# Stick-breaking attention in a four-layer trunk: the weight matrix taken as differences of one scan, the values as steps between neighbours

## The chip, the cores and the metric

The kernel runs on one core of one Trainium2 chip. The core has TensorE (PE, with its weight loads listed apart as PEld), VectorE (DVE), ScalarE (ACT), GpSimd (POOL) and the queue of SyncE (SP), which issues most of the transfers. The metric is the time of one execution in device microseconds (us); of several runs the median is taken.

## The reference

The program computes a trunk in float32 for a sequence of 1024 positions and a model width of 1024: a convolution layer, a gated feed-forward layer, an attention layer and a second feed-forward layer. The change touches the attention layer only. Its core, cut to what is computed:

```python
z = jnp.einsum("bhqd,bhsd->bhqs", q_blk, kf) * scale
valid = kpos[None, :] < qpos[:, None]
log_keep = jnp.where(valid, jax.nn.log_sigmoid(-z), 0.0)
rc = lax.cumsum(log_keep, axis=3, reverse=True)
after = jnp.concatenate([rc[..., 1:], jnp.zeros_like(rc[..., :1])], axis=-1)
weight = jnp.where(valid, jnp.exp(jax.nn.log_sigmoid(z) + after), 0.0)
return jnp.einsum("bhqs,bhsd->bhqd", weight.astype(v.dtype), v)
```

With keep = sigmoid(-z) and beta = sigmoid(z) = 1 - keep, a weight is beta at one key times the product of keep over all later keys before the query. There are 16 heads of width 64, and queries go in blocks of 128.

## The kernel before

All large tensors live in 1024-column slots of SBUF, given out by the class `Mem` from a first-in, first-out list. float32 products on PE are made from two rounded parts, a high part that ACT casts and a low part (value minus high part) that DVE subtracts; a full product is three matmuls (`mm3`).

Attention (`attention`, line 1384 on) works on pairs of heads, p = 0 to 7. For each pair there are these stages:

- `qkv_piece` multiplies 8 row tiles t by the pair's slice of the weights, 8 pieces k each. `qkv_split` prepares the next pair's weights: 8 casts on ACT (L1166) and 8 subtractions on DVE (L1167). `qkv_post` takes a finished tile out of PSUM: q and k by an ACT copy (L1190), the value part v by an ACT cast (L1193) and a DVE subtraction (L1194). `qkv_stat` squares on POOL (L1202), sums on DVE (L1203, then L709), takes a power on POOL (L710) and scales on POOL (L1212).
- `stacks` transposes q and k on PE (L1228) and splits the result: ACT L1234, DVE L1237.
- `z_part` makes the scores (L1260, L1261, and a mask matmul L1263). From PSUM, ACT writes keep (L1265) and beta (L1266).
- `z_scan` runs a product scan over keep, from the last key to the first, on DVE (L1274). `z_mul` multiplies beta by the scan, shifted by one column, on POOL (L1279).
- `a_bank` transposes the weights 128 by 128 on PE (L1293), casts the high part on ACT (L1297) and subtracts the low part on DVE (L1298). `av_bank` multiplies by v (L1312) and adds two halves (ACT L1322, DVE L1323).

The transposes of `stacks` and `a_bank` share two PSUM banks, called tr here. They take turns, so a transpose waits until the DVE instruction that reads the same bank two transposes earlier is done. The scores have two banks of their own.

What sets the order: PE's order in attention is written out by hand. Each step gets a time in units, 20 units to a pair, from tables at the end of `attention` (`ZT`, `ST`, `ZL` and others), and steps are issued in the order of these times. On DVE, ACT, POOL and SP a planner orders the instructions when the program is built, so a changed cost or dependence can move them. Each engine and each queue then works strictly in its order. After the tile t = 7 of a pair its v is complete; the first `av_bank` that reads it comes some 14 units later. Towards the end (`wo_start`) the output projection's weights are loaded and split beside the last pair, partly by POOL (L629 in `o_split`).

Of the kernel before, what the change touches and what calls it, by code (L numbers as in the profile page):

```python
# [618 lines left out]
class Kern:  # L619
# [563 lines left out]
    def qkv_post(self, p, t):  # L1183
        nc, m = self.nc, self.m
        ps = self.qps
        half, tl = divmod(t, 4)
        if tl == 0:
            self.qk[p, half] = m.alloc()
            self.V[p, half] = m.alloc()
        nc.scalar.copy(out=m.ap(self.qk[p, half])[:, tl * 256:(tl + 1) * 256], in_=ps[:, 0:256])  # L1190
        v = m.ap(self.V[p, half]).rearrange("p (t h c) -> p t h c", t=4, h=2)[:, tl]
        pv = ps[:, 256:384].rearrange("p (h c) -> p h c", h=2)
        nc.scalar.copy(out=r(v[:, :, 0:DH]), in_=pv)  # L1193
        nc.vector.tensor_tensor(out=r(v[:, :, DH:2 * DH]), in0=pv, in1=v[:, :, 0:DH], op=ALU.subtract)  # L1194
# [47 lines left out]
    def z_part(self, p, h, qb, c0):  # L1242
# [4 lines left out]
        if c0 == 0:  # L1247
            bs = m.alloc()
            if n <= 512:
                ks, B, K = None, m.ap(bs)[:, 0:n], m.ap(bs)[:, 512:512 + n]  # L1250
            else:
                ks = m.alloc()
                B, K = m.ap(bs)[:, 0:n], m.ap(ks)[:, 0:n]
            self.A[p, h, qb] = (bs, B, ks, K)
        _, B, _, K = self.A[p, h, qb]
# [8 lines left out]
        sc = DH ** -0.5  # L1264
        nc.scalar.activation(K[:, c0:c1], ps, AF.Sigmoid, scale=-sc)  # L1265
        nc.scalar.activation(B[:, c0:c1], ps, AF.Sigmoid, scale=sc)  # L1266
# [4 lines left out]
    def z_scan(self, p, h, qb):  # L1271
        K = self.A[p, h, qb][3]
        rev = K[:, 1:(qb + 1) * P][:, ::-1]
        self.nc.vector.tensor_tensor_scan(out=rev, data0=rev, data1=rev, initial=1.0, op0=ALU.mult, op1=ALU.bypass)  # L1274

    def z_mul(self, p, h, qb):
        bs, B, ks, K = self.A[p, h, qb]
        n = (qb + 1) * P
        self.nc.gpsimd.tensor_tensor(out=B[:, 0:n - 1], in0=B[:, 0:n - 1], in1=K[:, 1:n], op=ALU.mult)  # L1279
        if ks is not None:  # L1280
            self.m.free(ks)

    def a_bank(self, p, h, i, b):

        nc, m = self.nc, self.m
        q0, q1 = self.A[p, h, 2 * i], self.A[p, h, 2 * i + 1]
        ps = self.tr()
        pos, spans = 0, []
        for kb in (2 * b, 2 * b + 1):
            qs = (q0, q1) if kb <= 2 * i else (q1,)  # L1290
            spans.append((kb, pos, len(qs) * P))
            for q in qs:
                nc.tensor.transpose(ps[:, pos:pos + P], q[1][:, kb * P:(kb + 1) * P], self.ident)  # L1293
                pos += P
        s = m.alloc()
        aH, aL = m.ap(s)[:, 0:pos], m.ap(s)[:, 512:512 + pos]
        nc.scalar.copy(out=r(aH), in_=ps[:, 0:pos])  # L1297
        nc.vector.tensor_tensor(out=r(aL), in0=ps[:, 0:pos], in1=aH, op=ALU.subtract)  # L1298
        self.AT[p, h, i, b] = (s, spans)
        if b == i:  # L1300
            for q in (2 * i, 2 * i + 1):
                m.free(self.A.pop((p, h, q))[0])
# [81 lines left out]
    def attention(self):  # L1384
# [20 lines left out]
        for p in range(NP):  # L1405
# [16 lines left out]
            for h in range(2):  # L1422
                bh = base + U // 2 * h
                for qb, dt in enumerate(self.ZT):
# [4 lines left out]
                    for fn, lag in zip((self.z_scan, self.z_mul), self.ZL):  # L1429
                        at(bh + dt + lag, fn, p, h, qb)  # L1430
# [41 lines left out]
    ZL, ZC = (1.0, 1.035), 0.379  # L1472
# [41 lines left out]
    def run(self):  # L1514
        tc, nc, a = self.tc, self.nc, self.a
        with tc.tile_pool(name="ht", bufs=1) as hp, tc.tile_pool(name="cst", bufs=1) as cp, \
# [24 lines left out]
            nc.gpsimd.memset(self.mhalf, -0.5)  # L1541
            self.stat = cp.tile([P, 16], F32, name="stat")
# [4 lines left out]
            self.qk, self.V, self.stk, self.A, self.oT, self.oparts = {}, {}, {}, {}, {}, {}  # L1547
# [75 lines left out]
```

## Time and profile before

| quantity | value |
|---|---|
| time, median of 3 runs | 2319.72 us (2318.87 to 2321.71) |
| time of the profiled execution | 2319.02 us |
| span of the profiled execution | 2317.2 us |
| granted TensorE clock, mean | 0.993 |
| PE busy | 2232.6 us (96%) |
| DVE busy | 1726.5 us (75%) |
| ACT busy | 1262.6 us (54%) |
| POOL busy | 561.8 us (24%) |
| attention in the span | about 1055 to 1615 us |

The profiled execution spends 1.8 us outside its span. A row of the profile's timeline has the start in us, the duration in us, the engine, the line, the operation, output and input tiles, shape, count, and in brackets how long that engine had been idle before and which instruction ended the wait. Rows of equal kind that follow one another are merged, and then the duration is that of all. A row by group has busy time and the mean in nanoseconds of one. PE's durations overlap (a matmul of 512 columns is listed with 0.39 us, but the next starts 0.23 us after it), so a gap on PE is counted from the end that the profile models.

### The profile page before, as it was taken

Reading aid. Unit: us, or ns where it says so; the run is one execution under the profiler, and the core shown is the slowest. Engines: PE = TensorE matmul, PEld = TensorE weight load, DVE = VectorE, ACT = ScalarE, POOL = GpSimd, SP = SyncE. Lnnn points to the kernel's source line nnn. Section 1 sums busy time; section 2 is a strip of 40 time slices with the busy share of each in tenths; the row PEclk is TensorE's granted clock in tenths of the full one; section 3 lists DMA queues with packets and bytes.
Section 4 is the critical chain, followed back from the end, with each engine's and each line's share of the span. In section 5 each row is a group of like instructions: output and inputs, shape, how many; then the busy total and the mean of one; then the engine's idle time right before and its main releaser. Section 6 shows DMA issues by size and latency. Waiting matters only on the chain. (4 is left out here: it accounts for less than half of the span.)

```text
span 2317.2 us, 29706 instructions
## 1 busy us (share of the span) xinstructions
PE 2232.6 (96%) x11076; PEld 1908.4 (82%) x11076; DVE 1726.5 (75%) x2023; ACT 1262.6 (54%) x1978; POOL 561.8 (24%) x551
## 2 busy tenths in 40 slices
PE   8998999999999999999999999989999999999999
PEld 8886887888788888889999999978777888888887
DVE  6879457877686887556888888887668777778863
ACT  6433246555555543436677677765566565655341
POOL 2221012111111000035555555562121121110000
PEclk9999999999999999999999999999999999999999
DMA  5984146767676494321111110034476767666812
GB/s 178 190 174 99 35 127 144 191 144 193 148 186 155 146 386 168 103 80 28 37 28 37 37 37 10 28 106 152 130 162 166 192 149 196 145 177 249 332 51 109
DMA packets 247826, 313.00 MB, mean 135 GB/s; under 512 B 12557, under 2 KB 170753, under 8 KB 247681
## 3 DMA queue, kind: packets, MB, share of 16 engines
q1 hardware_dynamic: 214977, 238.32, 31.0%
q0 software_dynamic: 32704, 72.78, 17.7%
q8 instruction: 87, 1.43, 0.2%
q14 instruction: 58, 0.48, 0.1%
HBM read 181.14 MB, written 60.82 MB: 104 GB/s over the span
## 5 line engine op out<-in xcount | busy, mean ns | idle before, releaser
L199 POOL DMA_DIRECT2D t<-t x176 | 155.8, 978 | 701.2 <-ACT t L194 271.3
L628 ACT CAST t<-t 128x1024 fp32r<-128x1024 f32 x178 | 184.9, 1048 | 223.9 <-DMA hs<-t 62.0
L819 DVE SCALAR_TENSOR_TENSOR t<-t,cst,t 128x1023 f32<-128x1023 f32 (+1 forms) x184 | 236.1, 1286 | 81.9 <-ACT t L817 76.7
L629 DVE TENSOR_TENSOR t<-t,t 128x1024 fp32r<-128x1024 f32 x178 | 219.1, 1237 | 101.0 <-ACT t L628 47.2
L1274 DVE TENSOR_TENSOR_SCAN t<-t 128x127 f32<-128x127 f32 (+7 forms) x128 | 204.1, 1600 | 6.9 <-ACT t L1265 6.8
L644 PE MATMUL ps1s<-wH,hH 128*128 128x384 f32 x448 | 165.8, 370 | 0.0
L646 PE MATMUL ps0b<-hH,t 128*128 128x512 f32 x396 | 154.6, 391 | 3.5 <-DVE t L629 3.4
L644 PE MATMUL ps0b<-hH,t 128*128 128x512 f32 x396 | 155.8, 395 | 1.9 <-DVE t L1104 1.4
L645 PE MATMUL ps0b<-hL,t 128*128 128x512 f32 x396 | 154.7, 391 | 0.0
L710 POOL TENSOR_TENSOR stat<-stat,mhalf 128x8 f32<-128x8 f32 (+1 forms) x65 | 80.2, 1234 | 299.9 <-DVE stat L709 299.7
L646 PE MATMUL ps1s<-wH,hL 128*128 128x384 f32 x448 | 151.1, 337 | 0.0
L1279 POOL TENSOR_TENSOR t<-t,t 128x639 f32<-128x639 f32 (+1 forms) x64 | 108.6, 1697 | 175.1 <-DVE t L1274 103.7
L645 PE MATMUL ps1s<-wL,hH 128*128 128x384 f32 x448 | 150.9, 337 | 0.0
L817 ACT ACTIVATE t<-t,cst 128x1024 f32<-128x1024 f32 x88 | 109.1, 1240 | 66.3 <-DVE t L392 47.4
L645 PE MATMUL ps2b<-t,t 128*128 128x512 f32 x342 | 133.9, 392 | 3.9 <-DMA t<-t 3.9
L644 PE MATMUL ps2b<-t,t 128*128 128x512 f32 x342 | 134.0, 392 | 3.3 <-ACT t L394 1.6
L646 PE MATMUL ps2b<-t,t 128*128 128x512 f32 x342 | 132.7, 390 | 0.0
L1265 ACT ACTIVATE t<-ps1s 128x512 f32<-128x512 f32 (+1 forms) x192 | 95.4, 497 | 54.7 <-PE ps1s L1261 28.3
L1297 ACT CAST t<-ps1s 128x512 fp32r<-128x512 f32 (+1 forms) x160 | 87.3, 546 | 60.9 <-PE ps1s L1293 53.5
L1298 DVE TENSOR_TENSOR t<-ps1s,t 128x512 fp32r<-128x512 f32 (+1 forms) x160 | 100.2, 627 | 21.0 <-ACT t L1297 18.8
L517 ACT CAST hH<-t 128x1024 fp32r<-128x1024 f32 x64 | 64.4, 1051 | 86.4 <-PE ps0bs L645 19.6
L517 ACT CAST hL<-t 128x1024 fp32r<-128x1024 f32 x64 | 64.3, 1051 | 86.3 <-PE ps2s L645 25.3
(348 smaller groups left out, 6480.7 us busy)
## 6 DMA issues: line engine op xcount, KB each, us to landing
t<-in_ffn_w_up_dram SPq DMA_DIRECT2D x88, 512.0 KB
t<-t POOLq DMA_DIRECT2D x176, 256.0 KB, 4.4
t<-hs SPq DMA_DIRECT2D x66, 512.0 KB
hs<-t SPq DMA_DIRECT2D x60, 512.0 KB
t<-in_ffn_w_down_dram SPq DMA_DIRECT2D x66, 256.0 KB
xd<-t SPq DMA_DIRECT2D x24, 512.0 KB
wr<-in_attn_w_qkv_dram SPq DMA_DIRECT2D x24, 512.0 KB
t<-in_ffn_w_up_dram SPq DMA_DIRECT2D x44, 256.0 KB
```

What stands on the lines that cost most here:

```text
L199: nc.gpsimd.dma_start(out=out, in_=src, accum_op=ALU.add)
L517: nc.scalar.copy(out=r(m.ap(h)), in_=src)
L628: nc.scalar.copy(out=r(m.ap(h)), in_=m.ap(src))
L629: (eng or nc.vector).tensor_tensor(out=r(m.ap(l)), in0=m.ap(src), in1=m.ap(h), op=ALU.subtract)
L644: mm(out=ps, lhsT=sH, rhs=mH, start=start, stop=False, skip_group_check=onto)
L645: mm(out=ps, lhsT=sH, rhs=mL, start=False, stop=False, skip_group_check=onto)
L646: mm(out=ps, lhsT=sL, rhs=mH, start=False, stop=stop, skip_group_check=onto)
L817: nc.scalar.activation(dst, src, AF.Identity, scale=wcols[2], bias=bias)
L819: nc.vector.scalar_tensor_tensor(out=dst[:, s:], in0=src[:, :S - s], scalar=wcols[2 - s], in1=dst[:, s:], op0=ALU.mult, op1=ALU.add)
L1274: self.nc.vector.tensor_tensor_scan(out=rev, data0=rev, data1=rev, initial=1.0, op0=ALU.mult, op1=ALU.bypass)
L1279: self.nc.gpsimd.tensor_tensor(out=B[:, 0:n - 1], in0=B[:, 0:n - 1], in1=K[:, 1:n], op=ALU.mult)
L1298: nc.vector.tensor_tensor(out=r(aL), in0=ps[:, 0:pos], in1=aH, op=ALU.subtract)
```

## The change

The scan runs over all n columns of keep, not over columns 1 to n-1. Its result c[s] is the product of keep over keys s and later, and a weight is c[s+1] - c[s]. The sum of weights times v is summed by parts: it is the sum over s of (c[s] - 1) times (v[s-1] - v[s]), with v[-1] = 0. So beta and its product with the scan are gone, and v is replaced by the steps between neighbouring rows. The subtraction of one is made where the transposed weights leave PSUM: ACT adds a bias of -1, and DVE subtracts 1 and then the high part in one instruction. The steps of v cross partitions: v is first copied unsplit from PSUM into a slot `vr`; three transfers on SP write it, one row further down, into a slot `vs`; DVE subtracts; then ACT casts and DVE subtracts for the two parts, 512 columns at a time.

```diff
+        if t == 0:
+            self.vr[p] = m.alloc()
+        nc.scalar.copy(out=m.ap(self.qk[p, half])[:, tl * 256:(tl + 1) * 256], in_=ps[:, 0:256])
+        nc.scalar.copy(out=m.ap(self.vr[p])[:, t * P:(t + 1) * P], in_=ps[:, 256:384])
+        if t == NT - 1:
+            self.v_steps(p)
+
+    def v_steps(self, p):
+        nc, m = self.nc, self.m
+        vr, vs = self.vr.pop(p), m.alloc()
+        R, W = m.ap(vr), m.ap(vs)
+        nc.gpsimd.memset(W[0:1, 0:P], 0.0)
+        nc.sync.dma_start(out=W[1:113, :], in_=R[0:112, :])
+        nc.sync.dma_start(out=W[113:P, :], in_=R[112:P - 1, :])
+        nc.sync.dma_start(out=W[0:1, P:S], in_=R[P - 1:P, 0:S - P])
+        nc.vector.tensor_tensor(out=R, in0=W, in1=R, op=ALU.subtract)
+        m.free(vs)
+        for half in range(2):
             self.V[p, half] = m.alloc()
-        nc.scalar.copy(out=m.ap(self.qk[p, half])[:, tl * 256:(tl + 1) * 256], in_=ps[:, 0:256])
-        v = m.ap(self.V[p, half]).rearrange("p (t h c) -> p t h c", t=4, h=2)[:, tl]
-        pv = ps[:, 256:384].rearrange("p (h c) -> p h c", h=2)
-        nc.scalar.copy(out=r(v[:, :, 0:DH]), in_=pv)
-        nc.vector.tensor_tensor(out=r(v[:, :, DH:2 * DH]), in0=pv, in1=v[:, :, 0:DH], op=ALU.subtract)
+            v = m.ap(self.V[p, half]).rearrange("p (t h c) -> p t h c", t=4, h=2)
+            src = R[:, half * 512:(half + 1) * 512].rearrange("p (t h c) -> p t h c", t=4, h=2)
+            nc.scalar.copy(out=r(v[:, :, :, 0:DH]), in_=src)
+            nc.vector.tensor_tensor(out=r(v[:, :, :, DH:2 * DH]), in0=src, in1=v[:, :, :, 0:DH], op=ALU.subtract)
+        m.free(vr)
...
-        sc = DH ** -0.5
-        nc.scalar.activation(K[:, c0:c1], ps, AF.Sigmoid, scale=-sc)
-        nc.scalar.activation(B[:, c0:c1], ps, AF.Sigmoid, scale=sc)
+        nc.scalar.activation(K[:, c0:c1], ps, AF.Sigmoid, scale=-DH ** -0.5)
...
-        rev = K[:, 1:(qb + 1) * P][:, ::-1]
+        rev = self.m.ap(self.A[p, h, qb])[:, 0:(qb + 1) * P][:, ::-1]
...
-    def z_mul(self, p, h, qb):
-        bs, B, ks, K = self.A[p, h, qb]
-        n = (qb + 1) * P
-        self.nc.gpsimd.tensor_tensor(out=B[:, 0:n - 1], in0=B[:, 0:n - 1], in1=K[:, 1:n], op=ALU.mult)
-        if ks is not None:
-            self.m.free(ks)
...
-        nc.scalar.copy(out=r(aH), in_=ps[:, 0:pos])
-        nc.vector.tensor_tensor(out=r(aL), in0=ps[:, 0:pos], in1=aH, op=ALU.subtract)
+        nc.scalar.activation(r(aH), ps[:, 0:pos], AF.Identity, bias=self.mone[:, 0:1])
+        nc.vector.scalar_tensor_tensor(out=r(aL), in0=ps[:, 0:pos], scalar=1.0, in1=aH, op0=ALU.subtract,
+                                       op1=ALU.subtract)
...
-    ZL, ZC = (1.0, 1.035), 0.379
+    ZL, ZC = 1.0, 0.379
```

A query block's weights now take one slot where those of more than 512 columns took two. PE's order in attention is the same instruction by instruction. What moves stands on DVE, ACT, POOL and SP; the rows below are the program's order, not times, and a scan reads SCALAR_TENSOR_TENSOR in them. In the changed kernel L1208 is the subtraction that makes the steps, L1215 the low part of the steps, L1225 stands for L1203, L1259 for L1237, L1288 for the scan L1274, L1305 for L1298 and L1331 for L1323.

The first place is DVE around the transposes of `stacks` in a middle pair (1242 us in the profile before). The two tr banks are ps1s_7481 and ps1s_7482 before. Before:

```order
L1167 TENSOR_TENSOR wL<-wr,wH 128x384 x3
L1274 SCALAR_TENSOR_TENSOR t_9396<-t_9396 128x767
L1323 TENSOR_TENSOR t_9229<-ps1s_7475,tmp 64x256
L1298 TENSOR_TENSOR t_9423<-ps1s_7482,t_9423 128x512
L1167 TENSOR_TENSOR wL<-wr,wH 128x384 x2
L1194 TENSOR_TENSOR t_9180<-ps1s_7478,t_9180 128x2x64
L1167 TENSOR_TENSOR wL<-wr,wH 128x384
L1298 TENSOR_TENSOR t_9456<-ps1s_7481,t_9456 128x384
L1203 TENSOR_REDUCE stat_99<-tmp 128x4
L709 TENSOR_SCALAR stat_99<-stat_99 128x8
L1237 SCALAR_TENSOR_TENSOR t_9469<-ps1s_7482,cst,t_9469 64x512
L1237 SCALAR_TENSOR_TENSOR t_9471<-ps1s_7482,cst,t_9471 64x512
```

The same place after the change; the banks are ps1s_7486 and ps1s_7487, t_8749 is `vr`, t_9309 is `vs`:

```order
L1305 SCALAR_TENSOR_TENSOR t_9291<-ps1s_7487,t_9291 128x512
L1167 TENSOR_TENSOR wL<-wr,wH 128x384 x3
L1225 TENSOR_REDUCE stat_101<-tmp 128x4
L1305 SCALAR_TENSOR_TENSOR t_9334<-ps1s_7486,t_9334 128x384
L709 TENSOR_SCALAR stat_101<-stat_101 128x8
L1208 TENSOR_TENSOR t_8749<-t_9309,t_8749 128x1024
L1305 SCALAR_TENSOR_TENSOR t_9376<-ps1s_7486,t_9376 128x384
L1215 TENSOR_TENSOR t_9315<-t_8749,t_9315 128x8x64
L1215 TENSOR_TENSOR t_9318<-t_8749,t_9318 128x8x64
L1259 SCALAR_TENSOR_TENSOR t_9347<-ps1s_7487,cst,t_9347 64x512
L1259 SCALAR_TENSOR_TENSOR t_9349<-ps1s_7487,cst,t_9349 64x512
```

Four instructions (L1208, one L1305 and two L1215) now stand ahead of the pair L1259 that frees the bank of the stack's transposes; before, L1237 came straight after L709.

The second place is DVE at the start of attention, where pair 0's values are finished and its stacks begin (1051 us). Before:

```order
L1167 TENSOR_TENSOR wL<-wr,wH 128x384 x7
L1194 TENSOR_TENSOR t_7325<-ps0bb_548,t_7325 128x2x64
L1167 TENSOR_TENSOR wL<-wr,wH 128x384
L1203 TENSOR_REDUCE stat_99<-tmp 128x4
L709 TENSOR_SCALAR stat_99<-stat_99 128x8
L1237 SCALAR_TENSOR_TENSOR t_7513<-ps1s_7482,cst,t_7513 64x512
L1237 SCALAR_TENSOR_TENSOR t_7515<-ps1s_7482,cst,t_7515 64x512
```

After:

```order
L1167 TENSOR_TENSOR wL<-wr,wH 128x384 x7
L1167 TENSOR_TENSOR wL<-wr,wH 128x384
L1225 TENSOR_REDUCE stat_101<-tmp 128x4
L709 TENSOR_SCALAR stat_101<-stat_101 128x8
L1208 TENSOR_TENSOR t_7004<-t_7450,t_7004 128x1024
L1259 SCALAR_TENSOR_TENSOR t_7518<-ps1s_7487,cst,t_7518 64x512
L1259 SCALAR_TENSOR_TENSOR t_7520<-ps1s_7487,cst,t_7520 64x512
```

Here L1208, which waits for the three transfers, stands directly ahead of the first L1259.

The third place is ACT at the middle pair of the first place. Before:

```order
L1166 CAST wH<-wr 128x384
L1297 CAST t_9456<-ps1s_7481 128x384
L1234 ACTIVATE t_9469<-ps1s_7482,cst 64x512
L1234 ACTIVATE t_9471<-ps1s_7482,cst 64x512
L1265 ACTIVATE t_9485<-ps1s_7479 128x512
L1266 ACTIVATE t_9484<-ps1s_7479 128x512
L1297 CAST t_9500<-ps1s_7481 128x384
```

After:

```order
L1166 CAST wH<-wr 128x384
L1304 ACTIVATE t_9334<-ps1s_7486,mone 128x384
L1256 ACTIVATE t_9347<-ps1s_7487,cst 64x512
L1280 ACTIVATE t_9362<-ps1s_7484 128x512
L1304 ACTIVATE t_9376<-ps1s_7486,mone 128x384
L1214 CAST t_9315<-t_8749 128x8x64
L1214 CAST t_9318<-t_8749 128x8x64
L1256 ACTIVATE t_9349<-ps1s_7487,cst 64x512
```

L1214 is the cast of the steps, L1256 stands for L1234, L1280 for L1265 and L1304 for L1297. The two casts, which wait for L1208 on DVE, stand ahead of the second L1256; before, the two L1234 followed one another, and a beta activation (L1266) followed every L1265. On SP the three transfers of a pair stand ahead of the next load of weights.

24 lines of the change are left out of this document (9 added, 15 removed).

## The prediction

> **What bounds the kernel now.** I read the busy times by stretch, then PE's timeline for its gaps, then what DVE, POOL and ACT did ahead of each gap. From the transposes of one pair to those of the next (columns: stretch, its length, busy us and count of PE, PEld, DVE, ACT, POOL, granted clock, transfer share, GB/s):
>
> ```profile
> 1178.30:1245.94 67.64, 63.92 (x424) 61.76 (x425) 56.55 (x81) 49.03 (x112) 37.78 (x32) 1.00 0.11 32
> ```
>
> PE is busy 63.9 of 67.6 us, so about 3.7 us per pair can be won at most by shortening other engines' work. DVE is busy 56.6 us and strictly in order. ACT (49.0) and POOL (37.8), which the change relieves most, count only through DVE. The gaps of this pair, the next row in the same bank, and the last pair with the same picture:
>
> ```profile
> 1242.61 0.66 PE L1228 MATMUL ps1s<-ident,t 128*128 128x128 f32 x4 [1.54 <-DVE t L1298]
> 1244.46 0.34 PE L646 MATMUL ps1s<-wH,hL 128*128 128x384 f32 x1
> 1245.94 0.52 PE L1293 MATMUL ps1s<-ident,t 128*128 128x128 f32 x3 [0.68 <-DVE t L1298]
> 1248.80 0.60 PE L1293 MATMUL ps1s<-ident,t 128*128 128x128 f32 x4
> 1255.58 0.63 PE L1293 MATMUL ps1s<-ident,t 128*128 128x128 f32 x4 [0.39 <-DVE t L1237]
> 1259.78 0.66 PE L1293 MATMUL ps1s<-ident,t 128*128 128x128 f32 x4 [0.79 <-DVE t L1298]
> 1269.96 0.33 PE L1261 MATMUL ps1s<-t,t 128*128 128x128 f32 x1 [0.33 <-DVE t L1237]
> ...
> 1445.81 0.66 PE L1228 MATMUL ps1s<-ident,t 128*128 128x128 f32 x4 [1.54 <-DVE t L1298]
> ```
>
> Each ends on DVE. The sum is 1.54 + 0.68 + 0.39 + 0.79 + 0.33 = 3.73 us, and the pattern comes five times (first gap 1.54 to 1.75). Without gaps PE would be at the stack's transposes at 1241.07. An earlier pair had a longer first gap:
>
> ```profile
> 1106.98 1.11 PE L1228 MATMUL ps1s<-ident,t 128*128 128x128 f32 x4 [2.64 <-DVE t L1298]
> 1110.32 0.34 PE L646 MATMUL ps1s<-wH,hL 128*128 128x384 f32 x1
> ...
> 1105.00:1110.00 5.00, 3.02 (x10) 2.83 (x11) 5.00 (x8) 1.42 (x3) 2.43 (x2) 0.69 0.00 0
> ```
>
> After 2.64 us of idling the granted clock was 0.69 in those 5 us. From the transposes to the third L646 it took 3.34 us, where the middle pair took 1.85 (1242.61 to 1244.46). So this **dip cost 1.5 us** beside the gap; the gaps up to 1.75 us had none.
>
> **What the change removes, at the middle pair.** By count: 192 activations L1266 on ACT, 128 products L1279 on POOL, 64 DVE subtractions L1194.
>
> ```profile
> L1266 ACT ACTIVATE t<-ps1s 128x512 f32<-128x512 f32 (+1 forms) x192 | 94.9, 495 | 0.0
> L1279 POOL TENSOR_TENSOR t<-t,t 128x639 f32<-128x639 f32 (+1 forms) x64 | 108.6, 1697 | 175.1 <-DVE t L1274 103.7 <-ACT t L1266 23.2 <-PE ps1s L1312 11.8
> ...
> 1231.88 1.91 POOL L1279 TENSOR_TENSOR t<-t 128x383 f32<-128x383 f32 x2
> 1232.65 0.59 ACT L1266 ACTIVATE t<-ps1s 128x512 f32<-128x512 f32 x1
> 1233.27 0.93 ACT L1166 CAST wH<-wr 128x384 fp32r<-128x384 f32 x2
> 1234.39 0.42 DVE L1203 TENSOR_REDUCE stat<-tmp 128x4 f32<-128x256 f32 x1 [1.78 <-POOL tmp L1202]
> 1239.91 1.74 DVE L1274 TENSOR_TENSOR_SCAN t<-t 128x767 f32<-128x767 f32 x1
> L1167 DVE TENSOR_TENSOR wL<-wr,wH x64: 541/551/1405, 965.2 to 1448.0; 128x384 fp32r<-128x384 f32 x64
> ```
>
> DVE stood idle 1.78 us before L1203, since its POOL square (L1202) was queued behind two products that ended at 1233.79. Without them L1203 runs ahead of need, and DVE is held next by the ACT casts L1166, which move up by the 0.6 us of L1266: the first L1167 at about 1233.3. From there two L1167 (0.55 each alone), scan (1.5), L1298 (0.66), three L1167, scan (1.74) and L1323 (0.4) make 7.0 us: 1240.3. The new L1298 has one operation more. The nearest rows differ by 0.07 us (two rows below: 677 ns, against half of 1.51 us for a scalar form with half the partitions); I take 0.75, bounded by 0.68 and 0.82, so the bank is free at 1241.1. **The 1.54 us gap closes.** Three L1167, L1203 and the next L1298 end at 1243.75, and PE, shifted, is there at 1245.94 - 0.68 - 1.54 = 1243.72: **the 0.68 closes too**. The bias on ACT costs ACT up to 0.1 us more per cast; it has idle time, and if that cover were gone it would add 0.1 to the two gaps.
>
> **What it adds there.** After L709 (0.17, 1243.9) comes L1208, which waits for three transfers. Nearest prices:
>
> ```profile
> L629 DVE TENSOR_TENSOR t<-t,t 128x1024 fp32r<-128x1024 f32 x178 | 219.1, 1237 | 101.0 <-ACT t L628 47.2
> L1298 DVE TENSOR_TENSOR t<-ps1s,t 128x512 fp32r<-128x512 f32 x93 | 63.0, 677 | 5.6 <-ACT t L1297 4.9
> L524 ACT CAST t<-t 128x512 fp32r<-128x512 f32 x17 | 10.0, 618 | 5.8 <-DMA t<-hs 4.2 <-DVE t L525 1.1 <-DVE hL L518 0.3
> t<-t POOLq DMA_DIRECT2D x176, 256.0 KB, 4.4
> ...
> 1239.98 0.28 ACT L1193 CAST t<-ps1s 128x128 fp32r<-128x128 f32 x1
> 1246.36 1.51 DVE L1237 SCALAR_TENSOR_TENSOR t<-ps1s,cst,t 64x512 fp32r<-64x512 f32 x2
> ...
> 1508.10 0.32 SPq L1334 DMA_DIRECT2D t<-od  x1
> 1511.82 1.04 ACT L628 CAST hH<-t 128x1024 fp32r<-128x1024 f32 x1 [1.19 <-DMA t<-od]
> ```
>
> The last v tile leaves PSUM at 1240.26 (L1193, whose copy stays). SP issues at 0.32 us each, the large transfer second, so at about 1240.6. A 512 KB load issued at 1508.10 was waited for until 1511.82: 3.7 us. So landing is at 1244.3, and L1208, the price of an SBUF subtraction of 1024 columns (1.24), ends at 1245.55. L1305 (0.6) ends at 1246.15. Then the ACT casts L1214 (0.62 each from 1245.55, the second done 1246.8) and two L1215 (0.68 each, the DVE row of 512 columns) to 1247.6, and the pair L1259 (1.51, as L1237) to 1249.1. On ACT the second L1256 stands behind the casts and is done at 1247.5, in time for its L1259. Queued behind L1208 on DVE is thus all that frees tr banks, and PE waits for it: it used this bank at 1248.80, now shifted by 1.54 + 0.68 to 1246.6. **New gap: 2.5 us.** Of the later 1.51 us (0.39, 0.79, 0.33) I keep 0.3, between nothing and all, since DVE's waits for POOL and the L1266 between ACT's casts go there too. Gaps come to 2.8 instead of 3.73: minus 0.9. But 2.5 is nearest to the 2.64 row, so I charge a dip, 1.5 less 0.3 that later waits hide: **plus 0.3 per pair, times five, plus 1.5 us**. The first pair paid gap 2.64 and dip already (2.64 + 1.5 + the later 1.51 = 5.65, against 2.8 + 1.2 = 4.0): **minus 1.6**. POOL's memset of one partition and SP's three issues hold up no one: the load of weights behind them is first used a pair later.
>
> Bounds of a pair: the transfer between landing before L709 (gap 2.1) and 4.4 us, the median landing of the 256 KB transfers in the row above (gap 3.2); a collision of L1215 with POOL's L1212 between nothing and 0.9. That last is the lock seen here:
>
> ```profile
> 1062.45 0.42 DVE L1274 TENSOR_TENSOR_SCAN t<-t 128x127 f32<-128x127 f32 x1
> 1191.07 2.00 POOL L1279 TENSOR_TENSOR t<-t,t 128x1023 f32<-128x1023 f32 x1 [5.16 <-DVE t L1274]
> 1192.00 1.35 DVE L1274 TENSOR_TENSOR_SCAN t<-t 128x127 f32<-128x127 f32 x1
> ```
>
> The same scan took 0.42 alone and 1.35 under a product. I take no collision, as L1212 would start near 1245.6 and L1208 ends there.
>
> **The Trainium skill**, page "TensorE: Matmul & The Clock Gate", section "HAM oscillation — how this bites in real kernels", gives an idle window of about 3.4 us before the clock falls. By it a 2.5 us gap has no dip, and the five pairs would come to minus 4.5 instead of plus 1.5. The 2.64 us row above speaks against it.
>
> **Start, before attention and last pair.**
>
> ```profile
> 1039.73 0.44 PE L644 MATMUL ps0bb<-wH,hH 128*128 128x384 f32 x1 [0.98 <-DVE t L1194]
> 1049.88 0.27 ACT L1193 CAST t<-ps0bb 128x128 fp32r<-128x128 f32 x1
> 1054.69 0.63 PE L1228 MATMUL ps1s<-ident,t 128*128 128x128 f32 x4 [1.10 <-DVE t L1237]
> 1057.41 0.66 PE L1228 MATMUL ps1s<-ident,t 128*128 128x128 f32 x4 [1.03 <-DVE t L1237]
> ...
> 1522.08 1.77 POOL L1279 TENSOR_TENSOR t<-t,t 128x895 f32<-128x895 f32 x1
> 1522.79 0.55 PE L1293 MATMUL ps1s<-ident,t 128*128 128x128 f32 x3 [3.15 <-DVE t L1298]
> 1528.48 4.38 POOL L629 TENSOR_TENSOR hL<-t,hL 128x1024 fp32r<-128x1024 f32 x1
> 1531.21 2.73 DVE L629 TENSOR_TENSOR hL<-t,hL 128x1024 fp32r<-128x1024 f32 x1
> 1533.99 0.79 PE L645 MATMUL ps1s<-hL 128*128 128x512 f32 x1 [4.01 <-DVE hL L629]
> ```
>
> Pair 0: v is out at 1050.15, the large transfer is issued at 1050.6 and lands at 1054.3; L1208 to 1055.55, L1259 to 1057.1. The third stack goes from 1054.69 to 1057.1, plus 2.4. The next gap (1.03) is absorbed, leaving 1.4, and a gap of 3.5 dips (1.5): **plus 2.9**, bounded by 0 (early landing) and 4. Before it, PE waited for L1194 to free a bank; now the ACT copy frees it, about half a microsecond sooner: **minus 0.5**. In the last pair the 4.01 us gap hangs on L629, stretched to 2.73 by POOL's own L629 (4.38), which had queued behind the product at 1522.08 (1.77): **minus 2.0**. At 1522.79 the 3.15 us gap loses its cause, but L1208 and L1215 (2.6 us) come in there, behind transfers that share the queue with the output weights: 0. Bounds minus 8 to plus 4.
>
> **The sum:** +1.5 - 1.6 + 2.9 - 0.5 - 2.0 = +0.3 us on a span of 2317.2. The profiled execution took 2319.02, 0.7 below the median of the runs, so I predict 2319.7 + 0.3 = 2320.0. Feed-forward layers keep their work; only slots change, which I cost at nothing (bounds 3 either way).
>
> **Rivals.**
> - Gaps without dips: 1.2 less in six pairs and 1.5 at the start is 8.7 less: 2311.3. For it: gaps of 1.75 had none. Against: 2.64 had one. Chance 0.17. The window that the Trainium skill gives would have this result.
> - Relief goes through: landing before L709 (gap 2.1), no later gaps and no dip is 2.1 - 3.73 = minus 1.6 in five pairs, 2.1 - 5.65 = minus 3.6 in the first, 0 at the start, minus 0.5 before it, and the last pair at its bound, minus 8: minus 20, 2299.6. For it: POOL's waits in DVE are gone all through. Against: the row order puts 2.6 us of DVE work ahead of L1259 whatever lands when. Chance 0.17.
> - Slower: the steps come late. If L1259 ends over a microsecond later than 1249.1, by a landing of 4.4 (0.7) and the lock of L1215 (0.9), each pair pays 1.6 more, six times 9.6, the start 0.7 more and the last pair plus 2 instead of minus 2: 14.3, 2334.3. From about half a microsecond on it shows. For it: three transfers in a row and DVE in order. Against: L1212's slot. Chance 0.28.
>
> **How the numbers follow.** The forecast, a trade of old gaps for a new one, has 0.38, with 2315 to 2324 as its own range. Faster by over 0.2% (4.6 us, about what a measurement here can tell) are the first two rivals: 0.34. The range goes from 2302 to 2333.
>
> **What would show it.** Right: the product gone from POOL, the first two gaps of a pair gone, and one gap of 2 to 3 us at the second transposes after the stack, ended by L1259, with a granted clock below 1 behind it; L1208 waiting briefly for a transfer. The prediction would be wrong with no such gap, or gaps above 3.5 us; with L1208 waiting more than a microsecond; with a pair shorter than 66 or longer than 69.5 us.

## The result, and the profile after

| | before | after |
|---|---|---|
| median of the runs | 2319.30 us (4 runs, 2315.91 to 2321.71) | 2336.39 us (4 runs, 2333.25 to 2339.74) |
| profiled execution, its span | 2319.02, 2317.2 us | 2335.6, 2333.4 us |
| mean granted clock | 0.993 | 0.986 |

The changed kernel is slower: the ratio is 1.0075, with a 95% interval from 1.0056 to 1.0094. The prediction, 2320.0 us with a range up to 2333, missed it by 16 us and its range by 3. Medians are of undisturbed executions: one, of the kernel in "The relief alone", took 2466.40 us at a granted clock of 0.847 and is left out there.

The attention does in the main what the prediction said. First PE's gaps in two pairs of the changed kernel, from its timeline. In the new numbering L1250 are the stack's transposes, L1300 those of the weights, L1259 and L1305 the DVE instructions that free their banks:

```profile
1177.33 0.60 PE L1250 MATMUL ps1s<-ident,t 128*128 128x128 f32 x4
...
1179.74 0.49 PE L1300 MATMUL ps1s<-ident,t 128*128 128x128 f32 x3
...
1185.20 0.66 PE L1300 MATMUL ps1s<-ident,t 128*128 128x128 f32 x4 [2.44 <-DVE t L1259]
...
1195.56 0.66 PE L1300 MATMUL ps1s<-ident,t 128*128 128x128 f32 x4 [0.62 <-DVE t L1305]
...
1253.06 1.12 PE L1300 MATMUL ps1s<-ident,t 128*128 128x128 f32 x4 [3.75 <-DVE t L1259]
1253.83 0.67 PE L644 MATMUL ps1s<-wH,hH 128*128 128x384 f32 x1
1254.29 0.52 PE L645 MATMUL ps1s<-wL,hH 128*128 128x384 f32 x1
```

The first two gaps of a pair (1.54 and 0.68 us before) are gone, and one new gap stands where the tr bank of the second transposes is freed by L1259: 2.44 us in one pair, 3.75 in the next. After the second of them the transposes take 1.12 us instead of 0.66: the clock has dipped. Over the six pairs behind the first stacks the gap is 2.32 to 2.56 us in four and about 3.7 in two. DVE's timeline in the first pair shown has the chain that frees the bank, from the wait for the transfer at L1208 to L1259, with the scan behind it:

```profile
1178.80 0.16 DVE L709 TENSOR_SCALAR stat<-stat 128x8 f32<-128x8 f32 x1
1180.34 1.23 DVE L1208 TENSOR_TENSOR t<-t,t 128x1024 f32<-128x1024 f32 x1 [1.38 <-DMA t<-t]
1181.48 0.55 DVE L1305 SCALAR_TENSOR_TENSOR t<-ps1s,t 128x384 fp32r<-128x384 f32 x1
1182.25 1.36 DVE L1215 TENSOR_TENSOR t<-t,t 128x512 fp32r<-128x512 f32 x2 [0.22 <-ACT t L1214]
1183.63 1.52 DVE L1259 SCALAR_TENSOR_TENSOR t<-ps1s,cst,t 64x512 fp32r<-64x512 f32 x2
1185.18 2.02 DVE L1288 TENSOR_TENSOR_SCAN t<-t 128x896 f32<-128x896 f32 x1
```

In the next pair the transfer is waited for twice as long, and the chain ends later by nearly as much (1.3 us):

```profile
1248.27 1.23 DVE L1208 TENSOR_TENSOR t<-t,t 128x1024 f32<-128x1024 f32 x1 [2.77 <-DMA t<-t]
...
1251.49 1.51 DVE L1259 SCALAR_TENSOR_TENSOR t<-ps1s,cst,t 64x512 fp32r<-64x512 f32 x2
```

By stretches (columns as in the prediction: length, busy us and count of PE, PEld, DVE, ACT, POOL, granted clock, transfer share, GB/s), from the first of these gaps to the next pair's, and then 5 us around the end of the gap of 3.75 and of that of 2.44:

```profile
1185.20:1253.06 67.86, 63.49 (x425) 61.95 (x425) 52.79 (x76) 43.04 (x90) 16.44 (x17) 0.99 0.14 40
1251.00:1256.00 5.00, 2.94 (x12) 2.85 (x13) 4.69 (x5) 2.09 (x5) 0.38 (x1) 0.63 0.19 49
1185.00:1190.00 5.00, 4.80 (x32) 4.59 (x33) 3.49 (x5) 4.04 (x8) 0.69 (x1) 1.00 0.07 18
```

POOL is busy 16.4 us instead of 37.8, DVE 52.8 instead of 56.6, ACT 43.0 instead of 49.0, and the pair still takes 67.86 us against 67.64. So by these rows the attention is not where 16 us come from. I laid PE's 11076 instructions, which are the same in number and order, side by side in the two traces, and took the times (us) from one mark to the next. The marks are the first instruction, one close ahead of the attention, one at its end, a place shortly after the start of the second feed-forward layer, a place near its end, and the last instruction:

```
stage                              before     after    change
up to the attention                1018.3    1023.6     +5.3
attention                           637.8     639.3     +1.5
start of the second feed-forward    112.2     113.1     +0.9
second feed-forward layer           375.9     384.2     +8.3
the rest                            167.5     167.8     +0.3
```

The loss lies in layers whose instructions the change doesn't touch. What differs there is the matmuls themselves, at a granted clock of 1.00. One line of `mm3` between 600 and 640 us, before (columns after the count: min/median/max ns, first and last start):

```profile
L645 PE MATMUL ps0b<-hL,t x18: 389/389/389, 600.3 to 636.3; 128*128 128x512 f32 x18
...
L645 PE MATMUL ps0bs<-t,t x12: 389/389/389, 609.8 to 629.0; 128*128 128x512 f32 x12
```

and after:

```profile
L645 PEld LDWEIGHTS ps0b<-hL,t x19: 187/188/188, 601.1 to 638.6; 128*128 128x128 f32 x19
L645 PE MATMUL ps0b<-hL,t x19: 395/395/397, 601.3 to 638.8; 128*128 128x512 f32 x19
...
L645 PE MATMUL ps0bs<-t,t x12: 389/389/397, 611.7 to 631.4; 128*128 128x512 f32 x12
```

hH and hL are two large tiles of eight slots each, which lie ahead of the other slots; `t` is such a slot. A matmul whose operands are hL (or hH) and a slot is listed 6 ns longer; one with two slots is mostly as it was. In 200 us of the second feed-forward layer, before:

```profile
1800.00:2000.00 200.00, 199.66 (x880) 164.50 (x879) 154.53 (x160) 115.45 (x147) 36.89 (x42) 1.00 0.71 175
```

and after:

```profile
1800.00:2000.00 200.00, 197.97 (x854) 159.79 (x853) 145.18 (x150) 110.10 (x140) 34.74 (x40) 1.00 0.67 166
```

PE is busy nearly all the time in both, at full clock, and gets 854 matmuls through instead of 880 (the two stretches are some 8 us apart in the work).

### The profile page after: what moved, and what is told of

Same layout as the page of the kernel before. It is cut to its first block, busy times and chain, and to the rows that moved or that the text cites. A ratio compares the mean times of both kernels' runs of the same rounds, so it can differ in the third digit from the quotient of the medians.

```text
span 2333.4 us, 29165 instructions
## 1 busy us (share of the span) xinstructions
PE 2258.6 (97%) x11076; PEld 1920.8 (82%) x11076; DVE 1697.5 (73%) x1983; ACT 1216.2 (52%) x1802; POOL 384.5 (16%) x432
## 4 chain that ended last, share of the span: by engine, by line
PE 65%; DVE 6%; DMA 5%; ACT 3%; issue 2%; POOL 1%; SPq 0%; DVEq 0%; ACTq 0%; POOLq 0%
PE ps2b L644 7%; PE ps2b L645 7%; PE ps2b L646 7%; PE ps0b L644 4%; PE ps0b L645 4%; PE ps0b L646 4%; PE ps1s L644 3%; PE ps1s L646 3%; PE ps1s L645 3%; PE ps1s L1320 2%; PE ps1s L1300 2%; PE ps0bb L644 2%; PE ps0bb L645 2%; PE ps0bb L646 2%; DMA t<-t 2%
## 5 line engine op out<-in xcount | busy, mean ns | idle before, releaser
L629 DVE TENSOR_TENSOR t<-t,t 128x1024 fp32r<-128x1024 f32 x178 | 217.1, 1225 | 101.8 <-ACT t L628 43.5
L1288 DVE TENSOR_TENSOR_SCAN t<-t 128x128 f32<-128x128 f32 (+7 forms) x128 | 180.6, 1414 | 15.9 <-ACT t L1280 15.0
L644 PE MATMUL ps0b<-hH,t 128*128 128x512 f32 x396 | 158.2, 401 | 1.6 <-DVE t L1104 1.2
L646 PE MATMUL ps0b<-hH,t 128*128 128x512 f32 x396 | 157.1, 397 | 2.5 <-DVE t L629 2.5
L1304 ACT ACTIVATE t<-ps1s,mone 128x512 fp32r<-128x512 f32 (+1 forms) x160 | 103.4, 646 | 77.7 <-PE ps1s L1300 73.5
L1305 DVE SCALAR_TENSOR_TENSOR t<-ps1s,t 128x512 fp32r<-128x512 f32 (+1 forms) x160 | 100.8, 630 | 40.9 <-ACT t L1304 38.9
L1280 ACT ACTIVATE t<-ps1s 128x512 f32<-128x512 f32 (+1 forms) x192 | 93.3, 492 | 64.6 <-PE ps1s L1279 33.5
L710 POOL TENSOR_TENSOR stat<-stat,mhalf 128x8 f32<-128x8 f32 (+1 forms) x65 | 75.2, 1157 | 309.6 <-DVE stat L709 309.6
L1300 PE MATMUL ps1s<-ident,t 128*128 128x128 f32 x576 | 92.8, 280 | 20.6 <-DVE t L1259 17.1
```

The source lines that it names most:

```text
L629: (eng or nc.vector).tensor_tensor(out=r(m.ap(l)), in0=m.ap(src), in1=m.ap(h), op=ALU.subtract)
L644: mm(out=ps, lhsT=sH, rhs=mH, start=start, stop=False, skip_group_check=onto)
L646: mm(out=ps, lhsT=sL, rhs=mH, start=False, stop=stop, skip_group_check=onto)
L1300: nc.tensor.transpose(ps[:, pos:pos + P], q[:, kb * P:(kb + 1) * P], self.ident)
L1304: nc.scalar.activation(r(aH), ps[:, 0:pos], AF.Identity, bias=self.mone[:, 0:1])
```

## The experiments

**Theory M (memory addresses).** The change adds one small constant, `mone`, of one column. In the built program it takes 32 bytes per partition ahead of the slots. hH and hL (32768 bytes each) and the constants (6912) lie ahead of the first slot, which so begins 72448 bytes above hH in the kernel before, and 72480 in the changed one; all other slots move with it. The theory: a matmul of 512 columns is slower when its moving operand and the weights that are loaded beside it lie at different offsets. **Rivals:** changed slots and instruction order (S), or the attention's new gaps (G). Theory O, further down, is on the attention alone.

### The tile alone

```diff
             nc.gpsimd.memset(self.mhalf, -0.5)
+            self.mone = cp.tile([P, 1], F32, name="mone")
+            nc.gpsimd.memset(self.mone, -1.0)
```

> The kernel before with nothing but the new constant tile added (one column of -1.0, written once and never read). In the built program it moves every tile allocated behind it, all slots t16 to t53 among them, up by 32 bytes, so that they begin 32 bytes off a multiple of 64, while hH and hL stay on one. Theory M (a 512-column matmul is slower, about 233 instead of 227 ns, when its moving operand and the weights loaded beside it lie at different offsets within 64 bytes): 2331 to 2337 us, all of the loss in the feed-forward layers. Rival S (the loss comes from the changed slots and order of instructions) and rival G (it comes from the new gaps of the attention): 2317 to 2322 us, as the kernel before.

Measured: 2334.44 us (5 runs) beside 2323.07 of the kernel before (17 runs), ratio 1.0054 (1.0039 to 1.0068). An unused tile of one column costs 11.4 us. The same line as above, in this kernel:

```profile
L645 PE MATMUL ps0b<-hL,t x19: 395/396/397, 601.8 to 639.3; 128*128 128x512 f32 x19
...
L645 PE MATMUL ps0bs<-t,t x12: 389/389/398, 612.3 to 631.9; 128*128 128x512 f32 x12
```

It shows the changed kernel's durations without the change. S and G fall for the main part of the loss: 11.4 of some 17 us.

### The tile made 64 bytes wide

```diff
-            self.mone = cp.tile([P, 1], F32, name="mone")
+            self.mone = cp.tile([P, 16], F32, name="mone")
```

> The changed kernel with the new tile made 16 columns (64 bytes) wide, so that all slots lie on multiples of 64 bytes again; instructions and their order are the same. Theory M: 2319 to 2325 us, the 512-column matmuls of the feed-forward layers back at 227 ns, the attention as in the changed kernel. Rivals S and G: 2333 to 2340 us, as the changed kernel.

Measured: 2334.64 us (6 runs), ratio to before 1.0059 (1.0045 to 1.0074). Theory M failed as I had put it here: 64 bytes of shift cost as much as 32. The matmuls say why; they are still slow:

```profile
L645 PE MATMUL ps0b<-hL,t x16: 394/394/394, 604.2 to 639.6; 128*128 128x512 f32 x16
```

So either the offset counts over more than 64 bytes, or the address isn't the cause. The next four kernels decide that.

### All tiles moved together, and hH and hL moved alone

```diff
             self.cpool = cp
+            self.pad = hp.tile([P, 1], F32, name="pad")
             self.hH = hp.tile([P, KD, S], F32, name="hH")
```

This moves hH, hL and all slots by 32 bytes:

> The kernel before with an unused tile of 32 bytes ahead of hH, so that hH, hL and all slots move by 32 bytes together. Theory M (only a difference between the two operands costs): 2317 to 2323 us. Rival U (any operand that begins 32 bytes off a multiple of 64 costs): 2331 us or more.

With the unused tile `mone` behind the constants as well, the slots move by 64 bytes, and hH and hL by 32:

> The kernel before with an unused tile of 32 bytes ahead of hH and another behind the constants, so that hH, hL and the constants move by 32 bytes and the slots by 64: the difference between the operands is that of the first kernel of this group with its sides changed. Theory M: 2331 to 2337 us. Rival W (only weights that lie 32 bytes off cost): 2317 to 2322 us.

Measured: all moved together 2324.69 us (11 runs), ratio 1.0008 (0.9997 to 1.0019), no change. hH and hL moved against the slots: 2336.92 us (5 runs), ratio 1.0066 (1.0052 to 1.0081). Not where an operand lies costs, but how two operands lie to each other. Rivals U and W fall.

### The change without its tile, and a shift of 128 bytes

```diff
-            nc.gpsimd.memset(self.mhalf, -0.5)
-            self.mone = cp.tile([P, 1], F32, name="mone")
-            nc.gpsimd.memset(self.mone, -1.0)
+            nc.gpsimd.memset(self.mhalf[:, 0:15], -0.5)
+            nc.gpsimd.memset(self.mhalf[:, 15:16], -1.0)
```

with `bias=self.mhalf[:, 15:16]` in `a_bank`:

> The changed kernel without the new tile: its -1.0 stands in the last of the 16 columns of the tile that holds -0.5, of which at most 8 are read. Every tile lies where it lay in the kernel before; instructions are the same but for the start. Theory M, with the offset counted over at least 128 bytes (64 bytes of shift cost as much as 32): 2319 to 2326 us, the 512-column matmuls on hH and hL at 227 ns. Rivals S and G (slots, order or the attention's gaps): 2333 to 2340 us.

```diff
+            self.stat2 = hp.tile([P, 32], F32, name="stat2")
             self.hH = hp.tile([P, KD, S], F32, name="hH")
...
-            self.stat2 = cp.tile([P, 32], F32, name="stat2")
```

in the kernel before:

> The kernel before with the 128-byte tile of norms put ahead of hH: hH, hL and the constants move up by 128 bytes, the slots stay. Theory M with a period of 128 bytes: 2318 to 2326 us. Theory M with a longer period (256 bytes or more): 2331 to 2337 us.

Measured: the change without its tile takes 2323.65 us (11 runs) beside 2322.94 of the kernel before (17 runs), ratio 1.0002 (0.9993 to 1.0010). **The whole change in computation is worth nothing, and the 32 bytes that a constant takes are the rest.** The line in this kernel is back:

```profile
L645 PE MATMUL ps0b<-hL,t x19: 389/389/389, 600.6 to 637.3; 128*128 128x512 f32 x19
```

The shift of 128 bytes takes 2333.51 us (6 runs), ratio 1.0052 (1.0040 to 1.0064): slow as well. In the kernel before the slots begin 72448 bytes above hH, which is 283 times 256 but no multiple of 512, and slots lie multiples of 512 bytes apart. Both are fast. So of the distances seen, all multiples of 256 bytes are fast, and 32, 64 and 128 beside such a multiple are slow.

Behind the single lines stands this table, made from the times between the starts of successive 512-column matmuls in `mm3` (waits over 245 ns left out), sorted by where a matmul's moving operand (`rhs` in `mm3`; its weights are `lhsT`) and the next matmul's weights lie. Mean ns:

```
moving, next weights    before   +32    +64    +128   all +32   change without tile
hH or hL, slot           226.9   233.4  233.3  232.9   227.0     227.0
hH or hL, hH or hL       227.1   227.2  227.2  227.1   227.0     227.1
slot, slot               227.2   228.0  228.1  227.8   227.2     227.2
matmuls in first row      2953    2964   2965   2966    2942      2954
```

The columns +32 and +128 are the kernel before with one tile added or moved, +64 and the last are the changed program. 2964 matmuls at 6.5 ns more are 19 us; 10.6 to 13.9 us show in the three kernels before with a tile added or moved, and where the rest was absorbed I didn't trace.

### The relief alone

From here all kernels lack the new tile, so that addresses are those of before. The first stores V as before, with the product gone:

```diff
-        nc.scalar.copy(out=m.ap(self.vr[p])[:, t * P:(t + 1) * P], in_=ps[:, 256:384])
-        if t == NT - 1:
-            self.v_steps(p)
+        v = m.ap(self.V[p, half]).rearrange("p (t h c) -> p t h c", t=4, h=2)[:, tl]
+        pv = ps[:, 256:384].rearrange("p (h c) -> p h c", h=2)
+        nc.scalar.copy(out=r(v[:, :, 0:DH]), in_=pv)
+        nc.vector.tensor_tensor(out=r(v[:, :, DH:2 * DH]), in0=pv, in1=v[:, :, 0:DH], op=ALU.subtract)
```

> The kernel without the new tile and with V stored as it was before (no row steps; V itself is multiplied, so that part of the computation is left out): product, beta and their waits gone, nothing added to V. If the relief is real and only the V steps take it back: the gaps of 1.54 and 0.68 us of each pair go and no other comes, 2298 to 2308 us. Rival (other releasers fill the same gaps): 2315 to 2324 us.

Measured: 2292.74 us (3 runs), ratio 0.9873 (0.9859 to 0.9887): 30 us less, more than expected. The only gap of a pair, in two pairs of PE's timeline:

```profile
1182.56 0.65 PE L1278 MATMUL ps1s<-ident,t 128*128 128x128 f32 x4 [0.66 <-DVE t L1283]
...
1246.38 0.66 PE L1278 MATMUL ps1s<-ident,t 128*128 128x128 f32 x4 [0.66 <-DVE t L1283]
```

and the stretch from one to the other:

```profile
1182.56:1246.38 63.82, 63.16 (x424) 61.82 (x424) 52.40 (x81) 41.84 (x88) 16.18 (x17) 1.00 0.12 34
```

PE is busy 63.16 of 63.82 us. The V steps, where the change puts them, take 31 us (2323.65 less 2292.74).

### The V steps alone

The kernel before, its product kept, with `v_steps` added as in the change:

> The kernel before, its tiles in place and its product of beta kept, with the V steps of the change alone (the product runs on undiminished weights, so the output isn't the reference's: the summation by parts is left half done). If steps and relief simply add (product gone is worth 29 us, both together 0): 2345 to 2356 us, with the old gaps of a pair kept and the new one beside them. Rival: the wait for the product covers the V steps, as both fall in the same stretch of DVE's order: 2320 to 2335 us.

Measured: 2379.77 us (4 runs), ratio 1.0240 (1.0222 to 1.0258): 57 us, nearly twice what addition gave, so both readings missed. PE's timeline in a pair of this kernel:

```profile
1184.69 0.66 PE L1250 MATMUL ps1s<-ident,t 128*128 128x128 f32 x4 [1.51 <-DVE t L1320]
...
1197.72 1.09 PE L1315 MATMUL ps1s<-ident,t 128*128 128x128 f32 x4 [6.99 <-DVE t L1259]
```

and the pair's stretch:

```profile
1184.69:1259.97 75.28, 66.11 (x424) 63.97 (x425) 59.08 (x76) 50.14 (x114) 39.83 (x34) 0.95 0.13 36
```

The old gap of 1.51 us stays, the new one is 6.99 us, and a pair takes 75.28 us. The timeline of DVE and POOL ahead of such a gap (6.11 us) in an earlier pair:

```profile
1111.41 1.23 DVE L1208 TENSOR_TENSOR t<-t,t 128x1024 f32<-128x1024 f32 x1
...
1114.68 2.45 DVE L1296 TENSOR_TENSOR_SCAN t<-t 128x895 f32<-128x895 f32 x1 [0.19 <-ACT t L1287]
1117.05 2.83 DVE L1215 TENSOR_TENSOR t<-t,t 128x512 fp32r<-128x512 f32 x2
1117.36 1.98 POOL L1301 TENSOR_TENSOR t<-t,t 128x895 f32<-128x895 f32 x1 [2.11 <-DVE t L1296]
...
1120.64 1.53 DVE L1259 SCALAR_TENSOR_TENSOR t<-ps1s,cst,t 64x512 fp32r<-64x512 f32 x2 [0.75 <-ACT t L1256]
```

Two things lengthen the chain ahead of L1259: a scan (2.45) now stands inside it, and two L1215 take 2.83 us while POOL runs the product, against 1.36 in the changed kernel, where POOL was idle from 1182.46 us on. From the start of L1208 to the end of L1259 it takes 10.76 us here and 4.81 there; the two things make 3.9 of these 5.95 us, and most of the rest are longer waits of DVE for ACT. Thus relief and V steps do not add. That the same holds in every pair isn't shown, but six gaps on L1259 take 41 us of PE's time in this kernel.

### The wait for the transfer

The change without the moved rows:

```diff
-        nc.gpsimd.memset(W[0:1, 0:P], 0.0)
-        nc.sync.dma_start(out=W[1:113, :], in_=R[0:112, :])
-        nc.sync.dma_start(out=W[113:P, :], in_=R[112:P - 1, :])
-        nc.sync.dma_start(out=W[0:1, P:S], in_=R[P - 1:P, 0:S - P])
-        nc.vector.tensor_tensor(out=R, in0=W, in1=R, op=ALU.subtract)
+        nc.vector.tensor_tensor(out=R, in0=R, in1=R, op=ALU.add)
```

> The change without the new tile and without the moved rows: V is doubled in place instead of being subtracted from its moved copy, so the row step is left out; instructions of DVE and ACT for V stay as many, and no transfer is waited for. If DVE's wait for the transfer (1.3 us in the pair) is what makes the gap long enough for the half clock: gaps of about 1.2 us and no dips, 2300 to 2311 us. If the work alone does it: 2317 to 2325 us.

Measured: 2304.68 us (5 runs), ratio 0.9912 (0.9897 to 0.9927). PE's gaps in its timeline are 0.38, 0.49 and 0.15 us:

```profile
1181.42 0.65 PE L1246 MATMUL ps1s<-ident,t 128*128 128x128 f32 x4 [0.38 <-DVE t L1301]
...
1190.77 0.66 PE L1296 MATMUL ps1s<-ident,t 128*128 128x128 f32 x4 [0.49 <-DVE t L1301]
...
1241.72 0.55 PE L1296 MATMUL ps1s<-ident,t 128*128 128x128 f32 x3 [0.15 <-DVE t L1301]
```

So the first expectation came true. Of the 31 us of the V steps, 19 hang on the transfer (2323.65 less 2304.68). The gap vanished more fully than expected. The planner had a different program to order here, so part of that may be its new order.

### The V steps on POOL

```diff
-        nc.vector.tensor_tensor(out=R, in0=W, in1=R, op=ALU.subtract)
+        nc.gpsimd.tensor_tensor(out=R, in0=W, in1=R, op=ALU.subtract)
...
-            nc.scalar.copy(out=r(v[:, :, :, 0:DH]), in_=src)
-            nc.vector.tensor_tensor(out=r(v[:, :, :, DH:2 * DH]), in0=src, in1=v[:, :, :, 0:DH], op=ALU.subtract)
+            nc.gpsimd.tensor_copy(out=r(v[:, :, :, 0:DH]), in_=src)
+            nc.gpsimd.tensor_tensor(out=r(v[:, :, :, DH:2 * DH]), in0=src, in1=v[:, :, :, 0:DH], op=ALU.subtract)
```

> The kernel without the new tile, and with the three V steps (subtraction of the moved rows, cast, remainder) on POOL instead of DVE and ACT. Theory D (the gap of 2.3 to 3.7 us in each pair at the stack's transposes comes from the V steps standing ahead of the stack's casts on DVE): those gaps go, some 2.5 us and its half-clock time in 7 pairs, 2295 to 2306 us. Rival P (POOL now holds up the scaled q and k behind its wait for the transfer, and the gap only changes its releaser): 2317 to 2328 us.

Measured: 2358.00 us (4 runs), ratio 1.0152 (1.0139 to 1.0165), outside both expectations. The timeline of DVE and POOL ahead of a gap of 3.76 us on PE:

```profile
1110.27 2.39 POOL L1208 TENSOR_TENSOR t<-t,t 128x1024 f32<-128x1024 f32 x1
...
1111.01 3.53 DVE L1288 TENSOR_TENSOR_SCAN t<-t 128x896 f32<-128x896 f32 x1
1112.61 2.76 POOL L1234 TENSOR_TENSOR t<-t,stat 128x512 f32<-128x512 f32 x1
...
1114.57 1.53 DVE L1259 SCALAR_TENSOR_TENSOR t<-ps1s,cst,t 64x512 fp32r<-64x512 f32 x2
```

and the gap:

```profile
1116.16 1.12 PE L1300 MATMUL ps1s<-ident,t 128*128 128x128 f32 x4 [3.76 <-DVE t L1259]
```

The planner filled the freed place on DVE, ahead of L1259, with a scan of 896 columns, and that scan took 3.53 us beside POOL's work, where it takes 2.02 in the changed kernel with POOL at rest for nearly all of it. L1234, 2.76 us here, has a mean of 1.18 there. So at this gap, work moved from DVE to POOL came back as another DVE instruction in its place, and a longer one. Over the whole trace the weights' transposes (L1300) wait 37.8 us for L1259 in 12 gaps, against 18.1 in 7 in the change without its tile. How the 34 us divide between place and length isn't shown.

### The V steps held back

The transfers start where they did. Subtraction, cast and remainder run later, in two halves, each held behind the second half's stack:

```diff
+    def v_half(self, p, half):
+        one = self.stat[:, half:half + 1]
+        nc.vector.tensor_scalar(out=one, in0=m.ap(self.stk[p][0][2 * half])[:, 512:513], scalar1=0.0, scalar2=1.0,
+                                op0=ALU.mult, op1=ALU.add)
+        nc.vector.scalar_tensor_tensor(out=R, in0=W, scalar=one, in1=R, op0=ALU.mult, op1=ALU.subtract)
...
+                at(prev + self.VL[half] if p else -8.4 + 0.1 * half, self.v_half, p, half)
```

The factor 1.0 is computed from a value of the stack, so the planner cannot put the subtraction ahead of it.

> The whole change without the new tile, with the V steps held back: the subtraction and the remainder run in two halves, each behind the second half's stack casts on DVE (its factor 1.0 is made from a stack's column times zero plus one, so it cannot run ahead of it); the transfers are started where they were. Theory O (what costs is that the V steps stand ahead of the stack's casts and that DVE waits there for the transfer): the gaps of 2.3 to 3.7 us go, 2293 to 2306 us. Rival W (the 3.9 us of added work on DVE cost the same wherever they stand): 2315 to 2327 us.

Measured: 2295.14 us (4 runs, 2292.58 to 2300.67), ratio 0.9880 (0.9863 to 0.9897). **With all of the change's computation, this version is faster than both kernels, and than the one before by 1.2%.** DVE's timeline:

```profile
1184.24 0.69 DVE L1313 SCALAR_TENSOR_TENSOR t<-ps1s,t 128x512 fp32r<-128x512 f32 x1
...
1185.64 1.53 DVE L1267 SCALAR_TENSOR_TENSOR t<-ps1s,cst,t 64x512 fp32r<-64x512 f32 x2
1187.20 0.16 DVE L1214 TENSOR_SCALAR stat<-t 128x1 f32<-128x1 f32 x1
...
1188.33 0.74 DVE L1216 SCALAR_TENSOR_TENSOR t<-t,stat,t 128x512 f32<-128x512 f32 x1
...
1189.76 0.69 DVE L1221 TENSOR_TENSOR t<-t,t 128x512 fp32r<-128x512 f32 x1
```

PE's gap in its timeline, and the pair's stretch:

```profile
1184.99 0.66 PE L1308 MATMUL ps1s<-ident,t 128*128 128x128 f32 x4 [0.66 <-DVE t L1313]
```

```profile
1184.99:1249.28 64.29, 63.41 (x424) 61.82 (x424) 53.33 (x79) 42.87 (x90) 16.03 (x18) 1.00 0.14 42
```

The stack's DVE instructions (L1267) run first, no L1216 waits for a transfer, and the pieces (0.74 and 0.69) stand between casts instead of in one block. A pair takes 64.29 us, 0.5 more than with no V steps at all. DVE's work is 53.3 us, no less than in the changed kernel. So theory O holds: what cost was the place of the work and the wait, not its amount. Held back, the V steps cost 2.4 us (2295.14 less 2292.74); where the change puts them, but without the wait, 12 (2304.68 less 2292.74); with it, 31.

## Why the prediction was wrong

Point by point, by its steps:

- **The bound.** Right. PE bounds the attention, and its gaps could be won: with the product gone a pair falls from 67.64 to 63.82 us.
- **What the product's removal closes.** Right: the gaps of 1.54 and 0.68 are gone. The terms of relief come to about 25 us (3.73 less 0.3 in five pairs, 5.65 less 0.3 in the first, 0.5 and 2.0); the relief alone measured 30. L1305 was put at 0.75 us and is 0.69. The -2.0 of the last pair didn't show: the wait behind L629 is 3.56 us instead of 4.01, and the V steps, put at 0 in that place, cost: L1208 waits 1.04 us for its transfer there and takes 2.60, and PE stands idle 3.56 us until the L1305 behind it is done.
- **The new gap.** Right in place and releaser, and in four of six pairs in size: 2.5 forecast; 2.32 to 2.56 and about 3.7 in the trace. Counted from the pair's first L1250, L1208 was to start after 3.2 us and L1259 to end after 8.0; in the pair shown they did after 3.0 and 7.8 (1180.34 and 1185.15 less 1177.33). L1208's wait, though, is 1.38 us where I had 0.4, because DVE got there earlier; the end held, since the landing sets it. In the two pairs with the gap of 3.7 L1208 started after 4.2 and 4.4 us and L1259 ended after 9.1: the transfer landed later than priced, and why only there I didn't trace. By my own signs, a wait over a microsecond and a gap above 3.5 us, these rows count against the step.
- **The dips.** Charged at 1.2 us in each pair; they came behind five of the seven such gaps (clock 0.63 behind the gap of 3.75, 1.00 behind that of 2.44). Together gap and dips were to cost as much as the relief: 31 measured against 30. The forecast of a trade, +0.3 us, is borne out by the change without its tile: 2323.65 against 2322.94.
- **The sum of the attention.** Near the forecast, but in part by luck. Read between marks in the traces before and after (1018, 1074, 1142, 1480 and 1656 us of that before), the start costs 0.7 us more where 2.4 was forecast (2.9 less 0.5), the first pair 2.1 less (forecast 1.6 less), the five middle pairs together 0.1 more (forecast 1.5) and the last pair 2.8 more (forecast 2.0 less). The change without its tile has +0.6, -2.0, -0.5 and +3.1. The last pair came out some 5 us worse than forecast, and the others made up for most of it.
- **The step that failed:** "Feed-forward layers keep their work; only slots change, which I cost at nothing (bounds 3 either way)". They keep their work, but a new constant of one column moves the slots against hH and hL, and some 2960 matmuls take 6.5 ns longer from start to start. That is 10.6 to 13.9 us when done alone, in three ways, and in the change 13 us by the medians (2336.39 less 2323.65) or 17 by the two ratios (0.73%). The working priced every added instruction; where a tile lies was no term of it, and no reason was given for the nothing.

The slower rival named 2334.3, close to what came, but by another mechanism: L1259 was to end over a microsecond late in each pair, and it did so, by just over one, in two of six. The attention as a whole came out 1.2 us above the forecast (+1.5 against +0.3), not the 14.3 that this rival added to it.

The Trainium skill, page "TensorE: Matmul & The Clock Gate", section "HAM oscillation — how this bites in real kernels", was weighed with its window of about 3.4 us of idling. By it only the three gaps of about 3.7 should dip. The trace disagrees in part: gaps of 2.32 and 2.35 us dipped as well, and those of 2.44 and 2.56 did not. The first of these, in PE's timeline and in the 5 us behind it:

```profile
1117.98 0.66 PE L1300 MATMUL ps1s<-ident,t 128*128 128x128 f32 x4 [2.32 <-DVE t L1259]
```

```profile
1118.00:1123.00 5.00, 5.00 (x24) 4.78 (x25) 3.30 (x4) 4.15 (x8) 0.69 (x1) 0.66 0.03 8
```

## What to carry to other kernels

A new tile, however small, moves the tiles allocated behind it; before costing it at nothing, compare the addresses of matmul operands in the two built programs, and put a new constant into a free column of an old tile if they move against each other. When a change takes work from an engine and adds other work to it, price the place of the new work (what stands behind it, and what it waits for) ahead of its amount. If the planner lets an instruction run where it blocks its engine, a true dependence on what should go first moves it, at 0.16 us for each half here.

## What was not expected of the hardware

- Behind a 512-column matmul with its moving operand in hH or hL, when the next weights lie in a slot, the next matmul starts 6 to 6.5 ns later (after 233 instead of 227 ns) if the two lie 32, 64 or 128 bytes away from a multiple of 256 to each other; the weight loads are listed with 187 to 188 ns all the same. Which of PE's reads is held up isn't settled, and other distances weren't tried. The Trainium skill, page "SBUF — State Buffer", section "Operand start alignment", asks only for a multiple of the element's size, as a matter of legality and not of speed; the runs show that the time asks for more.
- DVE and POOL lengthened each other's instructions where both ran on SBUF: two L1215 took 2.83 instead of 1.36 us, a scan of 896 columns 3.53 instead of 2.02, POOL's L1234 2.76 instead of 1.18. The prediction had this for a scan under a product; that moving work from DVE to POOL would cost 34 us (2358.00 less 2323.65), by this and by the scan's new place, it had not.
- The stretches at half clock in the trace's clock records are 3.41 us long or a multiple of it (but for the last, which the end of the trace cuts off), and their starts lie a multiple of 3.41 us apart (two of them 58.03 us, 17 times). A gap's place against that grid decides whether it dips, as the kept traces show. In the changed kernel the gap of 2.32 us, which ends at 1117.98, falls into the one step of the grid from 1115.81 to 1119.22, PE is idle in 64% of that step, and the half clock starts at 1119.22. The gap of 2.44 is cut by the grid at 1184.08, idle in 39% of one step and 33% of the next, and doesn't dip. In the attention of all 13 traces, each of the 68 steps at full clock in which PE was idle for 55% or more (1.9 us) was followed by half clock, and no other was, with PE's ends as the profile models them. Outside the attention, between 45% and 54%, both came. The Trainium skill, page "TensorE: Matmul & The Clock Gate", section "What's actually happening", speaks of a free-running window of 4096 cycles at 1.2 GHz, 3413 ns; the trace agrees.
